# Moving 184 loads of a two-layer diffusion backbone from SyncE's DMA queue to GpSimd's, with the scan's loads fetched one job ahead

## The chip, the cores and the metric

One core of one Trainium2 chip. The metric is the device time of one execution of the whole program in microseconds (us); for this kernel the median of three runs is 2510.61 us, from 2509.51 to 2510.81 us.

## The reference, cut to what matters

Two layers work on 256 context tokens and 256 latent tokens of width 1024. Each layer is a half-step FFN, a mixer and a second half-step FFN; the change lies in the mixer alone.

```python
p = n @ w_in                                   # conv input, q/k/v, z, decay inputs, two gates
y = a * sigmoid(gate)                          # conv branch: depthwise conv of 31 taps along rows of 64
y_conv = silu(layernorm(dwconv(y, 31) + b)) @ conv_proj
# DeltaNet branch: q, k, v by a short conv; chunked scan in both directions, 8 heads of 128
v_new = u - w @ S
o     = (q * exp(g)) @ S + qk @ v_new          # qk = (q k^T) * decay
S     = S * exp(g_last) + (k * exp(g_last - g))^T @ v_new
y_dn  = (rms(o) * silu(z)) @ dn_proj
h    += gate2 * ((sigmoid(gA) * y_conv + sigmoid(gB) * y_dn) @ w_out)
```

Layer 0 produces both streams after the mixer, layer 1 the latent stream alone, so in layer 1 most products have 256 columns where those of layer 0 have 512.

## The kernel before, in words

Everything is kept with channels on the 128 partitions. Every fp32 product is three TensorE products of a high and a low part (`mm3`, L142). A weight tile of 512 KB (`raw`) is loaded by SyncE (L119), split into `whi` by ScalarE (L112) and `wlo` by VectorE (L113). There are three `raw` buffers and three pairs of `whi` and `wlo`, so the weights run at most six tiles ahead of TensorE.

A mixer (`mixer`) runs in these stages:

- The projections of `w_in`. The gated conv input is stored to DRAM (`glu`, L924), and so are `z` and the two gates `ga` and `gb` (from ScalarE's queue, L953). The logs of the decays go through DRAM (`grow`, L496) and come back broadcast over the partitions by eight accumulating DMAs of 512 KB on GpSimd's queue (`R<-grow`, L511); ScalarE takes their exponential in place (L513).
- The depthwise conv (`conv`, L810 to L824). For each of eight channel tiles the input `cx` is read back from `glu` with halos, in layer 0 by five DMAs, in layer 1 by one. VectorE then works through 31 taps (L824). Two `cx` buffers.
- The Gram matrices, and the block-wise inverses of the triangular systems.
- The scan (`scan`). Sixteen jobs, each one chunk of 128 tokens, one direction and four heads; the order alternates over two halves of the heads and two directions. Stages of different jobs are emitted side by side: `prepare` for the job three ahead, `residue` two ahead, `load` and `values` one ahead, `update` for the job itself. `load` reads the masked products `pt` (L739), the broadcast decays `qt` (L743) and the queries `q` (L745), 256 KB each, and VectorE multiplies `qt` by `q` (L746). `pt` and `qt` have two buffers, `q` one. `update` multiplies `qt` with the state `S` (L777) and `pt` with the new values (L778). In layer 1 only the eight jobs of the latent stream have outputs, and so these loads.
- `out_norm`: the outputs are normalised (a power on GpSimd, L883), transposed (L891) and multiplied by `z` (L892), which is loaded again (L888) into three buffers shared by all heads.
- `branch`: products with `conv_proj` and `dn_proj`, multiplied by the gates `g` (L1018). The first branch is stored (`m`, L1023), the second loads it again as `other` (L1009) and adds it (L1020). `g`, `other` and other temporaries share the four buffers `w512`.
- `w_out` and the residual.

A framework orders the instructions of each engine by priority and writes the waits. Each engine's instructions, SyncE's DMA issues included, then run strictly in their order; a DMA that waits for a buffer or for data holds back what stands behind it on its queue. The queues of SyncE, ScalarE and GpSimd move their bytes over the same 16 DMA engines.

Of the kernel before, what the change touches and what calls it, by code (L numbers as in the profile page):

```python
# [46 lines left out]
class Net:  # L47
# [660 lines left out]
    def scan(self, y, S, R, K, qsp, V, o, psp, pool, beside):  # L708


        nc = self.nc
        tile = lambda name, bufs: pool.tile([128, 4, 128], F32, tag=name, name=name, bufs=bufs)
# [15 lines left out]
        def load(g):  # L728
            if not g.last:
                g.kd = tile("kd", 2)  # L730
                pk = self.psx()
                for j in range(4):
                    nc.tensor.transpose(pk[:, j * 128:(j + 1) * 128], K[g.st][:, g.q * 4 + j, g.tok], self.ident)
                for j in range(4):
                    h = g.q * 4 + j
                    nc.scalar.activation(out=g.kd[:, j, :], in_=pk[:, j * 128:(j + 1) * 128], func=AF.Copy, scale=y.kd[:, g.d, g.t, h:h + 1])
            if g.need_o:
                g.pt = tile("pt", 2)
                nc.sync.dma_start(out=g.pt.rearrange("p h i -> p (h i)"), in_=psp[g.t][:, g.d * 1024 + g.q * 512:g.d * 1024 + g.q * 512 + 512])  # L739
                if not g.first:  # L740
                    g.qt, q = tile("qt", 2), tile("q", 1)
                    c0 = g.d * 32 + g.t * 8 + g.q * 4
                    nc.sync.dma_start(out=g.qt.rearrange("p h i -> p (h i)"),  # L743
                                      in_=y.rows[1][c0:c0 + 4, :].rearrange("a b -> (a b)").partition_broadcast(128))
                    nc.sync.dma_start(out=q, in_=qsp[g.st].rearrange("p (h t) -> p h t", h=8)[:, g.hs, g.tok])  # L745
                    nc.vector.tensor_tensor(out=g.qt, in0=g.qt, in1=q, op=ALU.mult)  # L746

        def residue(g):
# [41 lines left out]

        n = len(jobs)
        for i in range(-3, n):
            for off, stage in ((3, prepare), (2, residue), (1, load), (1, values), (0, update)):
                if 0 <= i + off < n:
                    stage(jobs[i + off])
            for f in beside.get(i, ()):
                f()

    def conv(self, y, glu, ysp, ysum, pool, tok):

        nc = self.nc
        ctx = tok.start == 0
        for k in range(KT):
            x = pool.tile([128, 8, 94], F32, tag="cx", name="cx")
            r0 = 0 if ctx else 4
            if ctx:
                c = glu[k][:, 0:256]
                nc.gpsimd.memset(x[:, 0, 0:15], 0.0)
                nc.gpsimd.memset(x[:, 3, 79:94], 0.0)
                nc.sync.dma_start(out=x[:, 0, 15:94], in_=c[:, 0:79])  # L810
                for r in (1, 2):
                    nc.sync.dma_start(out=x[:, r, :], in_=c[:, 64 * r - 15:64 * r + 79])
                nc.sync.dma_start(out=x[:, 3, 0:79], in_=c[:, 177:256])
            nc.gpsimd.memset(x[:, 4:, 0:15], 0.0)
            nc.gpsimd.memset(x[:, 4:, 79:94], 0.0)
            nc.sync.dma_start(out=x[:, 4:, 15:79], in_=glu[k][:, 256:512].rearrange("p (r c) -> p r c", c=64))
            o = pool.tile([128, 512], F32, tag="cy", name="cy")
            dst = o[:, tok].rearrange("p (r c) -> p r c", c=64)
            for j in range(31):
                w, src = y.cdw[:, j, k:k + 1], x[:, r0:, j:j + 64]  # L820
                if j == 0:
                    nc.vector.tensor_scalar(out=dst, in0=src, scalar1=w, scalar2=y.dwb[:, k:k + 1], op0=ALU.mult, op1=ALU.add)
                else:
                    nc.vector.scalar_tensor_tensor(out=dst, in0=src, scalar=w, in1=dst, op0=ALU.mult, op1=ALU.add)  # L824
            nc.sync.dma_start(out=ysp[k][:, tok], in_=o[:, tok])
            if k == 0:
                nc.vector.tensor_copy(out=ysum[:, tok], in_=o[:, tok])
            else:
                nc.vector.tensor_tensor(out=ysum[:, tok], in0=ysum[:, tok], in1=o[:, tok], op=ALU.add)
# [38 lines left out]
    def out_norm(self, y, o, s, zsp, oh, ol):  # L868

        nc = self.nc  # L870
        st, ts = STREAM[s], slice(2 * s, 2 * s + 2)
        so = self.sp.tile([128, 2, 8], F32, tag="so", name="so")
        for q in range(2):
            hs = slice(4 * q, 4 * q + 4)
            for tt in range(2):
                for h in range(4 * q, 4 * q + 4):
                    sq = self.wk.tile([128, 256], F32, tag="sq", name="osq", bufs=2)[:, :128]
                    nc.scalar.activation(out=sq, in_=o[:, 2 * s + tt, h, :], func=AF.Square, accum_out=so[:, tt, h:h + 1])
            sv, rq = so[:, :, hs], y.rq[:, ts, hs]
            nc.vector.tensor_tensor(out=sv, in0=sv, in1=rq, op=ALU.mult)  # L880
            nc.vector.scalar_tensor_tensor(out=sv, in0=sv, scalar=1.0 / 128, in1=rq, op0=ALU.mult, op1=ALU.mult)
            nc.vector.tensor_scalar(out=sv, in0=sv, scalar1=EPS, scalar2=None, op0=ALU.add)
            nc.gpsimd.tensor_tensor(out=sv, in0=sv, in1=self.mhalf[:, :8].rearrange("p (t h) -> p t h", t=2), op=ALU.pow)  # L883
            nc.vector.tensor_tensor(out=sv, in0=sv, in1=rq, op=ALU.mult)
            nc.vector.tensor_tensor(out=o[:, ts, hs, :], in0=o[:, ts, hs, :], in1=sv.unsqueeze(3).to_broadcast([128, 2, 4, 128]), op=ALU.mult)
            for h in range(4 * q, 4 * q + 4):
                z = self.wk.tile([128, 256], F32, tag="t1", name="z", bufs=3)
                nc.sync.dma_start(out=z, in_=zsp[h][:, st])  # L888
                ps = self.psx()
                for tt in range(2):  # L890
                    nc.tensor.transpose(ps[:, tt * 128:(tt + 1) * 128], o[:, 2 * s + tt, h, :], self.ident)  # L891
                nc.vector.scalar_tensor_tensor(out=z, in0=ps[:, :256], scalar=y.onorm, in1=z, op0=ALU.mult, op1=ALU.mult)  # L892
                self.split(oh[:, h, st], ol[:, h, st], z)

    def mixer(self, y, nxt):
        nc, a, l = self.nc, self.a, y.l
        w_in = a["w_in"][l]
        streams = (0, 1) if l == 0 else (1,)
        tok = FULL if l == 0 else STREAM[1]
        dram = lambda name, cols: self.dp.tile([128, cols], F32, name=f"{name}_{l}")  # L900
        hsp = dram("hsp", KT * T)
        psp = [dram(f"psp{t}", 2048) for t in range(4)]
        qsp = [dram(f"q{s}", 2048) for s in range(2)]
        zsp, asp, bsp, glu, ysp, msp = ([dram(f"{nm}{k}", T) for k in range(8)] for nm in ("z", "ga", "gb", "glu", "y", "m"))
        x, xctx = self.n, self.np_ctx
# [11 lines left out]
        for k in range(KT):  # L917
# [3 lines left out]
            t_ = self.w512("glu")  # L921
# [84 lines left out]

        def load(src, name):
            t_ = self.w512(name)
            nc.sync.dma_start(out=t_[:, tok], in_=src[:, tok])  # L1009
            return t_[:, tok]  # L1010

        oh, ol, mh, ml = [None] * 4
# [123 lines left out]
```

## Time and profile before

| | |
|---|---|
| median of three runs | 2510.61 us |
| the profiled execution | 2517.16 us |
| its span, first to last instruction | 2515.4 us |
| TensorE busy | 2410.1 us (96%) |
| VectorE busy | 1774.5 us (71%) |
| ScalarE busy | 956.0 us (38%) |
| GpSimd busy, without its DMA issues | 51.7 us (2%) |
| mean granted TensorE clock | 0.984 |
| moved by SyncE's queue | 371.33 MB |
| moved by GpSimd's queue | 8.39 MB |

The mixer of layer 0 lies between about 420 and 1060 us of the span, that of layer 1 between about 1830 and 2310 us; the FFNs fill the rest. SPq, POOLq and ACTq are the DMA issues of SyncE, GpSimd and ScalarE. "<-" in brackets names what ended the idle time before an instruction. Busy time of TensorE counts modelled ends, so a full slice is not TensorE at its peak.

### The profile page before, as it was taken

How to read it: one execution, taken by the hardware profiler on the slowest of the kernel's cores; microseconds unless marked ns; L12 is line 12 of the kernel's file. 1: busy time of each engine (PE TensorE's matmuls, PEld its weight loads, DVE VectorE, ACT ScalarE, POOL GpSimd, SP SyncE). 2: the span in 40 equal slices, each digit the busy share in tenths (PEclk: the TensorE clock that was granted, in tenths of full speed). 3: DMA queues.
4: the chain of work that ended last, by engine and by line, in shares of the span. 5: the costliest groups of instructions: out<-in, count | busy, mean ns of one | idle time of the engine just before them, and what ended most of it. 6: DMA issues, size and time to landing. Idle time of an engine off the chain costs nothing. (4 is left out here: it accounts for less than half of the span.)

```text
span 2515.4 us, 38318 instructions
## 1 busy us (share of the span) xinstructions
PE 2410.1 (96%) x15099; PEld 2043.3 (81%) x15099; DVE 1774.5 (71%) x3023; ACT 956.0 (38%) x1578; POOL 51.7 (2%) x111
## 2 busy tenths in 40 slices
PE   7999999999999999999999999999988998978998
PEld 5777778787887887887777888778887886878998
DVE  4766777699999665576667564444468999966554
ACT  3222222435443643332222232222245556544443
POOL 0000000100000000000000000000010000000000
PEclk9999999999999999999999999999999999988999
DMA  8556665744644474455555544444466572355664
GB/s 253 165 164 175 173 176 172 170 133 113 207 137 118 145 224 151 116 156 158 163 157 160 152 126 126 126 125 133 120 173 178 169 218 79 108 174 164 198 184 138
DMA packets 566773, 394.61 MB, mean 157 GB/s; under 512 B 27704, under 2 KB 513218, under 8 KB 564930
## 3 DMA queue, kind: packets, MB, share of 16 engines
q1 hardware_dynamic: 555606, 371.33, 51.2%
q0 software_dynamic: 2304, 8.39, 1.7%
q10 hardware_dynamic: 8684, 12.45, 1.5%
q8 instruction: 118, 1.93, 0.3%
q14 instruction: 61, 0.50, 0.1%
HBM read 358.43 MB, written 33.69 MB: 156 GB/s over the span
## 5 line engine op out<-in xcount | busy, mean ns | idle before, releaser
L142 PE MATMUL pm<-nh,whi 128*128 128x512 f32 (+1 forms) x2544 | 907.8, 359 | 23.2 <-ACT whi L112 16.3
L142 PE MATMUL pm<-nh,wlo 128*128 128x512 f32 (+1 forms) x2544 | 903.3, 356 | 2.9 <-DVE wlo L113 2.2
L142 PE MATMUL pm<-nl,whi 128*128 128x512 f32 (+1 forms) x2544 | 903.3, 356 | 0.0
L112 ACT ACTIVATE whi<-raw 128x1024 fp32r<-128x1024 f32 (+1 forms) x450 | 469.1, 1044 | 1109.3 <-PE pm L142 857.7
L113 DVE TENSOR_TENSOR wlo<-raw,whi 128x1024 fp32r<-128x1024 f32 (+1 forms) x450 | 541.1, 1204 | 237.3 <-ACT whi L112 233.2
L142 PEld LDWEIGHTS pm<-nh,whi 128*128 128x128 f32 x2544 | 480.9, 190 | 115.1 <-ACT whi L112 25.1
L142 PEld LDWEIGHTS pm<-nh,wlo 128*128 128x128 f32 x2544 | 480.9, 189 | 79.2 <-DVE wlo L113 4.4
L142 PEld LDWEIGHTS pm<-nl,whi 128*128 128x128 f32 x2544 | 481.3, 190 | 73.6 <-DVE nl L375 1.0
L296 DVE SCALAR_TENSOR_TENSOR aacc<-adaw,sc,aacc 128x512 f32<-128x512 f32 x448 | 312.3, 747 | 164.8 <-DMA adaw<-ada_w_in 164.7
L824 DVE SCALAR_TENSOR_TENSOR cy<-cx,cdw,cy 128x512 f32<-128x512 f32 (+1 forms) x480 | 272.0, 612 | 1.3
L142 PE MATMUL pm<-gh,whi 128*128 128x512 f32 (+1 forms) x770 | 268.8, 349 | 1.7 <-DVE h L380 1.7
L142 PE MATMUL pm<-gl,whi 128*128 128x512 f32 (+1 forms) x770 | 267.4, 347 | 0.0
L142 PE MATMUL pm<-gh,wlo 128*128 128x512 f32 (+1 forms) x770 | 267.3, 347 | 0.0
L142 PEld LDWEIGHTS pm<-gh,whi 128*128 128x128 f32 x770 | 145.7, 189 | 26.4 <-issue 3.4
L142 PEld LDWEIGHTS pm<-gh,wlo 128*128 128x128 f32 x770 | 145.7, 189 | 18.9 <-issue 0.8
L142 PEld LDWEIGHTS pm<-gl,whi 128*128 128x128 f32 x770 | 145.7, 189 | 17.6
L428 DVE TENSOR_TENSOR silu<-silu,pm 128x512 f32<-128x512 f32 (+1 forms) x88 | 54.5, 619 | 77.3 <-PE pm L142 70.2
L380 DVE SCALAR_TENSOR_TENSOR h<-pm,gate,h 128x256 f32<-128x256 f32 x80 | 36.4, 480 | 63.3 <-PE pm L142 63.0
L112 ACT ACTIVATE gh<-silu 128x512 fp32r<-128x512 f32 (+1 forms) x88 | 50.5, 573 | 39.1 <-DVE silu L428 39.0
L374 ACT ACTIVATE nh<-t,mods 128x256 fp32r<-128x256 f32 x88 | 39.9, 502 | 61.1 <-DVE t L371 61.0
L113 DVE TENSOR_TENSOR gl<-silu,gh 128x512 fp32r<-128x512 f32 (+1 forms) x88 | 54.4, 618 | 0.0
L142 PE MATMUL pm<-mh,whi 128*128 128x256 f32 (+1 forms) x152 | 48.3, 320 | 2.2 <-ACT mh L112 2.2
(248 smaller groups left out, 2376.9 us busy)
## 6 DMA issues: line engine op xcount, KB each, us to landing
raw<-ffn_w_in SPq DMA_DIRECT2D x208, 512.0 KB, 4.1
adaw<-ada_w_in SPq DMA_DIRECT2D x144, 512.0 KB, 4.0
raw<-w_in_in SPq DMA_DIRECT2D x130, 512.0 KB, 4.2
raw<-ffn_w_in SPq DMA_DIRECT2D x64, 448.0 KB, 4.3
R<-grow POOLq DMA_DIRECT2D x16, 512.0 KB, 13.9
raw<-conv_proj_in SPq DMA_DIRECT2D x16, 512.0 KB, 6.5
raw<-dn_proj_in SPq DMA_DIRECT2D x16, 512.0 KB
raw<-w_out_in SPq DMA_DIRECT2D x16, 512.0 KB, 4.1
```

The lines of the kernel that those rows point to most:

```text
L112: nc.scalar.activation(out=hi, in_=x, func=AF.Copy)
L113: nc.vector.tensor_tensor(out=lo, in0=x, in1=hi.bitcast(F32), op=ALU.subtract)
L142: nc.tensor.matmul(ps, lhsT=u[:, j, :], rhs=v[:, k, tok], start=k == 0 and p == 0, stop=k == n - 1 and p == 2)
L296: nc.vector.scalar_tensor_tensor(out=st.acc[:, s], in0=wt[:, j], scalar=c, in1=st.acc[:, s], op0=ALU.mult, op1=ALU.add)
L374: nc.scalar.activation(out=nh[:, k, st], in_=t1, func=AF.Identity, bias=B)
L380: self.nc.vector.scalar_tensor_tensor(out=self.h[:, m, st], in0=ps[:, st], scalar=y.gate[:, q, m, s:s + 1], in1=self.h[:, m, st], op0=ALU. ...
L428: nc.vector.tensor_tensor(out=t, in0=t, in1=pb[:, tok], op=ALU.mult)
L824: nc.vector.scalar_tensor_tensor(out=dst, in0=src, scalar=w, in1=dst, op0=ALU.mult, op1=ALU.add)
```

## The change

184 loads go from SyncE's queue to GpSimd's: 48 of `cx` (40 in layer 0), 24 of `pt`, 20 of `qt`, 20 of `q`, 24 of `z`, 32 of `g` and 16 of `other`. Weights, and all stores, stay where they were. In the scan, the loads become a stage of their own, `fetch`, which is emitted ahead of `residue`, for the job one ahead, and `q` gets a second buffer.

```diff
@@ scan
                     nc.scalar.activation(out=g.kd[:, j, :], in_=pk[:, j * 128:(j + 1) * 128], func=AF.Copy, scale=y.kd[:, g.d, g.t, h:h + 1])
+
+        def fetch(g):
             if g.need_o:
                 g.pt = tile("pt", 2)
-                nc.sync.dma_start(out=g.pt..., in_=psp[g.t][...])
+                nc.gpsimd.dma_start(out=g.pt..., in_=psp[g.t][...])
                 if not g.first:
-                    g.qt, q = tile("qt", 2), tile("q", 1)
+                    g.qt, q = tile("qt", 2), tile("q", 2)
-                    nc.sync.dma_start(out=g.qt..., in_=y.rows[1][...].partition_broadcast(128))
+                    nc.gpsimd.dma_start(out=g.qt..., in_=y.rows[1][...].partition_broadcast(128))
-                    nc.sync.dma_start(out=q, in_=qsp[g.st]...)
+                    nc.gpsimd.dma_start(out=q, in_=qsp[g.st]...)
                     nc.vector.tensor_tensor(out=g.qt, in0=g.qt, in1=q, op=ALU.mult)
-            for off, stage in ((3, prepare), (2, residue), (1, load), (1, values), (0, update)):
+            for off, stage in ((3, prepare), (1, fetch), (2, residue), (1, load), (1, values), (0, update)):
@@ conv: the four halo loads of the context and the one of the latent rows
-                nc.sync.dma_start(out=x[...], in_=glu[k][...])
+                nc.gpsimd.dma_start(out=x[...], in_=glu[k][...])
@@ out_norm
-                nc.sync.dma_start(out=z, in_=zsp[h][:, st])
+                nc.gpsimd.dma_start(out=z, in_=zsp[h][:, st])
@@ mixer, load of g and other
-            nc.sync.dma_start(out=t_[:, tok], in_=src[:, tok])
+            nc.gpsimd.dma_start(out=t_[:, tok], in_=src[:, tok])
```

The order on TensorE, VectorE and ScalarE hardly moves; SyncE and GpSimd are where it does. Line numbers of the changed kernel are two higher from the scan's loads on.

SyncE before the change, in the scan of layer 1. The eight jobs of the latent stream are called 1 to 8; `q_18953` is the q of job 4, `qt_18995`, `pt_18993` and `q_18996` belong to job 5, `qt_19038`, `pt_19036` and `q_19039` to job 6, and `y7`, `yc` to the conv branch:

```order
L745 DMA q_18953<-q1_1_14804 128x4x128
L743 DMA qt_18995<-grow11_15149 128x512
L739 DMA pt_18993<-psp2_1_14801 128x512
L745 DMA q_18996<-q1_1_14804 128x4x128
L825 DMA y7_1_14844<-cy_18486 128x256
L743 DMA qt_19038<-grow11_15149 128x512
L739 DMA pt_19036<-psp2_1_14801 128x512
L845 DMA yc_19118<-y0_1_14837 128x256
L845 DMA yc_19122<-y1_1_14838 128x256
L845 DMA yc_19128<-y2_1_14839 128x256
L745 DMA q_19039<-q1_1_14804 128x4x128
```

The q of a job is the last of its loads, behind the qt and pt of the same job and, for job 6, behind three loads of the conv branch.

GpSimd in the changed kernel, the same place: `qt_18880` and `pt_18878` are of job 3, `pt_18931` and `qt_18933` of job 4, `q_18987`, `qt_18986` and `pt_18984` of job 5, `q_19030`, `qt_19029` and `pt_19027` of job 6, `q_19062` of job 7:

```order
L745 DMA qt_18880<-grow11_15149 128x512
L741 DMA pt_18878<-psp2_1_14801 128x512
L747 DMA q_18987<-q1_1_14804 128x4x128
L741 DMA pt_18931<-psp3_1_14802 128x512
L745 DMA qt_18933<-grow11_15149 128x512
L745 DMA qt_18986<-grow11_15149 128x512
L741 DMA pt_18984<-psp2_1_14801 128x512
L747 DMA q_19030<-q1_1_14804 128x4x128
L745 DMA qt_19029<-grow11_15149 128x512
L741 DMA pt_19027<-psp2_1_14801 128x512
L747 DMA q_19062<-q1_1_14804 128x4x128
```

The q of a job now stands ahead of the qt and pt of its own job, for job 5 also ahead of those of job 4, and no load or store of the conv branch stands between.

GpSimd in the changed kernel, where the decays of layer 0 are read back (`R`); before the change only the power of L342 stood ahead of the `R` rows:

```order
L342 TENSOR_TENSOR rs_3297<-ms_3295,mhalf_91 128x2
L812 DMA cx_6797<-glu0_0_3367 128x79
L814 DMA cx_6797<-glu0_0_3367 128x94 x2
L815 DMA cx_6797<-glu0_0_3367 128x79
L818 DMA cx_6797<-glu0_0_3367 128x4x64
L812 DMA cx_6841<-glu1_0_3368 128x79
L814 DMA cx_6841<-glu1_0_3368 128x94 x2
L815 DMA cx_6841<-glu1_0_3368 128x79
L818 DMA cx_6841<-glu1_0_3368 128x4x64
L511 DMA R0_3394<-grow00_3681 128x1024 x4
L511 DMA R1_3395<-grow00_3681 128x1024 x4
```

Ten loads of the conv's first two channel tiles now stand ahead of the eight `R` loads; in layer 1 it is two.

## Rows read from the trace of the kernel before

**Rows 1.** The page, part 1: busy time, share of the span, instructions.

```profile
PE 2410.1 (96%) x15099; PEld 2043.3 (81%) x15099; DVE 1774.5 (71%) x3023; ACT 956.0 (38%) x1578; POOL 51.7 (2%) x111
```

**Rows 2.** Busy time by stretch: PE, PEld, DVE, ACT, POOL, granted clock, DMA share, GB/s.

```profile
940.00:980.00 40.00, 35.34 (x163) 27.93 (x164) 21.71 (x43) 13.03 (x46) 3.27 (x2) 0.90 0.51 160
1880.00:1900.00 20.00, 8.65 (x40) 7.95 (x41) 6.61 (x11) 8.90 (x11) 1.56 (x2) 0.67 0.98 220
2190.00:2216.00 26.00, 18.59 (x123) 17.44 (x122) 17.24 (x48) 8.18 (x29) 0.00 (x0) 0.84 0.75 234
2254.00:2278.00 24.00, 23.52 (x200) 23.32 (x200) 15.11 (x25) 9.12 (x12) 0.00 (x0) 1.00 0.86 250
```

**Rows 3.** Waits of ScalarE in time order, decays of layer 1 (start, us, instruction).

```profile
1872.17 1.06 ACT L513 ACTIVATE R<-R 128x1024 f32<-128x1024 f32 x1 [4.47 <-DMA R<-grow]
...
1894.66 1.06 ACT L112 ACTIVATE whi<-raw 128x1024 fp32r<-128x1024 f32 x1 [7.54 <-DMA raw<-w_in_in]
```

**Rows 4.** Waits of TensorE, 2186 to 2222 us (us in total, times, longest).

```profile
PE px L777 <- issue: 4.5, 2, 4.0
PE px L777 <- DVE qt L746: 2.7, 2, 2.3
```

**Rows 5.** VectorE in order of time, scan of layer 1.

```profile
2199.98 0.69 DVE L746 TENSOR_TENSOR qt<-qt,q 128x512 f32<-128x512 f32 x1 [2.75 <-DMA q<-q]
...
2211.38 0.69 DVE L746 TENSOR_TENSOR qt<-qt,q 128x512 f32<-128x512 f32 x1 [2.32 <-DMA q<-q]
```

**Rows 6.** SyncE's queue in order of time, scan of layer 1.

```profile
2194.81 0.37 SPq L745 DMA_DIRECT2D q<-q  x1
...
2206.51 0.37 SPq L745 DMA_DIRECT2D q<-q  x1
```

**Rows 7.** TensorE in order of time: first L777 of jobs 4, 5, 8.

```profile
2190.65 0.46 PE L777 MATMUL px<-S,qt 128*128 128x128 f32 x2 [0.55 <-issue]
...
2194.61 0.49 PE L777 MATMUL px<-S,qt 128*128 128x128 f32 x2
...
2212.17 0.77 PE L777 MATMUL px<-S,qt 128*128 128x128 f32 x2 [4.00 <-issue]
```

**Rows 8.** Waits of TensorE, 930 to 980 us.

```profile
PE px L891 <- DVE z L892: 4.5, 5, 1.5
PE px L777 <- DVE qt L746: 2.9, 1, 2.9
```

**Rows 9.** DMA issues of the whole span: count, KB each, median us to landing.

```profile
qt<-grow SPq DMA_DIRECT2D x20, 256.0 KB, 4.0
q<-q SPq DMA_DIRECT2D x20, 256.0 KB, 3.0
...
z<-z SPq DMA_DIRECT2D x24, 128.0 KB, 3.8
...
other<-m SPq DMA_DIRECT2D x8, 128.0 KB, 3.4
```

**Rows 10.** Tile R, 1855 to 1912 us: GpSimd's issues (ns min/median/max), landings (us).

```profile
L511 POOL DMA_DIRECT2D R<-grow x8: 862/898/1567, 1866.0 to 1884.1; - x8
...
DMA to landing us min/median/max: 6.2/12.0/17.0
```

**Rows 11.** Tile R, 440 to 510 us: GpSimd's issues in layer 0.

```profile
L511 POOL DMA_DIRECT2D R<-grow x8: 1578/2244/3400, 465.3 to 469.8; - x8
```

**Rows 12.** SyncE's queue, 440 to 505 us: loads of the conv's second tile.

```profile
462.06 0.54 SPq L810 DMA_DIRECT2D cx<-glu  x1
```

**Rows 13.** SyncE's queue, 2140 to 2320 us: first and last of eight loads of other.

```profile
2257.78 0.42 SPq L1009 DMA_DIRECT2D other<-m  x1
...
2282.78 0.58 SPq L1009 DMA_DIRECT2D other<-m  x1
```

More of the change, by code (lines that the diff above doesn't have):

```diff
@@ L736, in load @@
                     nc.scalar.activation(out=g.kd[:, j, :], in_=pk[:, j * 128:(j + 1) * 128], func=AF.Copy, scale=y.kd[:, g.d, g.t, h:h + 1])
+        def fetch(g):
             if g.need_o:
                 g.pt = tile("pt", 2)
-                nc.sync.dma_start(out=g.pt.rearrange("p h i -> p (h i)"), in_=psp[g.t][:, g.d * 1024 + g.q * 512:g.d * 1024 + g.q * 512 + 512])
+                nc.gpsimd.dma_start(out=g.pt.rearrange("p h i -> p (h i)"), in_=psp[g.t][:, g.d * 1024 + g.q * 512:g.d * 1024 + g.q * 512 + 512])
                 if not g.first:
-                    g.qt, q = tile("qt", 2), tile("q", 1)
+                    g.qt, q = tile("qt", 2), tile("q", 2)
                     c0 = g.d * 32 + g.t * 8 + g.q * 4
-                    nc.sync.dma_start(out=g.qt.rearrange("p h i -> p (h i)"),
+                    nc.gpsimd.dma_start(out=g.qt.rearrange("p h i -> p (h i)"),
                                       in_=y.rows[1][c0:c0 + 4, :].rearrange("a b -> (a b)").partition_broadcast(128))
-                    nc.sync.dma_start(out=q, in_=qsp[g.st].rearrange("p (h t) -> p h t", h=8)[:, g.hs, g.tok])
+                    nc.gpsimd.dma_start(out=q, in_=qsp[g.st].rearrange("p (h t) -> p h t", h=8)[:, g.hs, g.tok])
                     nc.vector.tensor_tensor(out=g.qt, in0=g.qt, in1=q, op=ALU.mult)
@@ L809, in conv @@
                 nc.gpsimd.memset(x[:, 3, 79:94], 0.0)
-                nc.sync.dma_start(out=x[:, 0, 15:94], in_=c[:, 0:79])
+                nc.gpsimd.dma_start(out=x[:, 0, 15:94], in_=c[:, 0:79])
                 for r in (1, 2):
-                    nc.sync.dma_start(out=x[:, r, :], in_=c[:, 64 * r - 15:64 * r + 79])
-                nc.sync.dma_start(out=x[:, 3, 0:79], in_=c[:, 177:256])
+                    nc.gpsimd.dma_start(out=x[:, r, :], in_=c[:, 64 * r - 15:64 * r + 79])
+                nc.gpsimd.dma_start(out=x[:, 3, 0:79], in_=c[:, 177:256])
             nc.gpsimd.memset(x[:, 4:, 0:15], 0.0)
             nc.gpsimd.memset(x[:, 4:, 79:94], 0.0)
-            nc.sync.dma_start(out=x[:, 4:, 15:79], in_=glu[k][:, 256:512].rearrange("p (r c) -> p r c", c=64))
+            nc.gpsimd.dma_start(out=x[:, 4:, 15:79], in_=glu[k][:, 256:512].rearrange("p (r c) -> p r c", c=64))
             o = pool.tile([128, 512], F32, tag="cy", name="cy")
```

## Prediction

> **What bounds the kernel now.** I begin with busy time. TensorE counts 96% of the span [rows 1], so a load that lands earlier is worth something only where TensorE stands still for it. The table by stretch shows where that is in the mixers [rows 2]: two stretches of the scans and what follows them (940 to 980 us in layer 0, 2190 to 2216 us in layer 1, with TensorE busy for 35.3 of 40 and 18.6 of 26 us), and the stretch in which the decays of layer 1 are read back (8.7 of 20 us).
>
> The views of waits then say who is late. In the decay stretch ScalarE, whose instructions run in order, waits 4.47 us for an `R` load and later 7.54 us for a weight [rows 3], while the 16 DMA engines are 0.98 busy: bytes are short there, not issue slots, and the change moves no byte away. In layer 1's scan, TensorE waits 4.5 and 2.7 us ahead of L777 [rows 4]. VectorE in order of time names the cause: the product of `qt` and `q` (L746) waits for `q`, twice [rows 5]. It can't come earlier: `q` has one buffer, so its load is issued only when the product before has ended, 2206.51 us for the product that starts at 2211.38 us [rows 5, 6]. SyncE's order in the section on the change shows the same: a q comes last, and behind what the conv branch wants. In layer 0 the like wait is 2.9 us, and the transposes wait another 4.5 us for `z` [rows 8].
>
> **The sum, against the profiled execution's 2517.16 us**, which is 6.55 us above the median of 2510.61 us.
>
> *Scan of layer 1.* With two buffers q is asked for a job earlier, and nothing of the conv branch stands before it. Undisturbed, job 5 follows job 4 by 2194.61 - 2190.65 = 3.96 us [rows 7]. At that pace job 8 starts 3 x 3.96 = 11.9 us after job 5, at 2206.5 us, and not at 2212.17 us: 5.7 us. Can `qt` follow? Its load waits for L777 two jobs before, then lands in 4.0 us from SyncE [rows 9]; the product takes 0.69 us [rows 5] and the 16 products L777 and L778 about 1.8 us, 123 matmuls being 13.8 us at 0.112 us each. That is 6.5 us for two jobs, under 7.9 us: it can. The granted clock there is 0.84 [rows 2], so 32% of 26 us, 8.3 us, ran at 1.2 GHz and cost 4.2 us. The low clock comes after these stalls, but idle time behind the scan stays; I take half, 2.1 us. Together **-7.8 us**. Bounds: no clock and a landing of 6.2 us as the quickest `R` load [rows 10], which is twice the bytes and adds on the way: 6.2 + 0.69 + 1.8 = 8.7 us for two jobs, job 8 at 2207.7 us, -4.5 us; the whole clock, -9.9 us.
>
> *Scan of layer 0.* The 2.9 us at L777 [rows 8] go, as the loads no longer queue behind stores of `m` that wait for VectorE: **-2.9 us** (bounds 0 and -6.9 us, with the 4.0 us that 40 us at a clock of 0.90 cost). The other loads of this scan lie beside products of `conv_proj`: nothing.
>
> *The decays.* GpSimd gets ten `cx` loads ahead of the `R` loads in layer 0. Those of the first tile are long gone; the five of the second can go once its `glu` has landed, which was so at 462.06 us [rows 12]. GpSimd's issues followed each other by (469.8 - 465.3) / 7 = 0.64 us, and one alone took 0.862 us [rows 10, 11]. Five take 3.2 to 4.3 us and end at 465.3 to 466.4 us; the first `R` load went at 465.3 us. In layer 1 it is one load. No cover here: ScalarE stands still for `R`. **+0.5 us** for both. Upper bound: the `cx` loads with four runs a partition could cost as four, 3.4 us each, so +3.7 and +3.4 us; lower bound 0.
>
> *z, g and other.* Three buffers for `z`, four for `g` and `other`: each load waits for the use of an older one, so landing time is on the path when TensorE has nothing else. The loads of `other` in layer 1 come (2282.78 - 2257.78) / 7 = 3.57 us apart [rows 13], where 24 products of a branch need 24 / 200 x 24 = 2.9 us [rows 2]: loads set the pace. I take the landing as unchanged, for the nearest rows are the same loads from SyncE, 3.4 and 3.8 us [rows 9], and price it at **0**. Bounds: at q's 3.0 us and at `R`'s 6.2 us. `other` makes 4 rounds (eight branches, two in flight), `z` 2 rounds in layer 1 (five loads behind the first three) and 4.3 in layer 0, of which I count half, as products of other branches run beside them: 4 x 2.8 + 4.2 x 2.4 = +21.3 us above, 4 x 0.4 + 4.2 x 0.8 = -5.0 us below.
>
> *Weights and conv input.* Six tiles of weights are ready or on their way, so SyncE's waits for loads were covered already; `cx` has two buffers and 31 taps of time. If that cover goes, in the decay stretch, the missing thing is bytes. Nothing.
>
> Sum: -7.8 - 2.9 + 0.5 = **-10.2 us**: 2507.0 us profiled, **2500.4 us** median.
>
> The quickest landing from GpSimd's queue in these rows is 6.2 us, for an accumulating load [rows 10]; no row has a plain one. The Trainium skill (DMA: Bandwidth & Descriptors, section Specifications) speaks against the change: first byte about 1 us on GpSimd's path and about 0.6 us on SyncE's. By that, an estimate, 0.4 us in each of the 8.2 rounds costs 3.3 us, and the sum would be -6.9 us, 2503.7 us; that plain loads are so slow no run here shows yet.
>
> **The rivals.**
>
> *Slower: landing.* If a plain load from GpSimd lands in 6.2 us, `z` and `other` pay 21.3 us, the scans give 4.5 + 2.9 us and the decays take 0.5 us: +14.4 us, **2525.0 us**. It decides from 10.2 / 8.2 = 1.2 us a landing on. For it: the only loads of that queue landed in 6.2 to 17.0 us [rows 10]. Against: they were 512 KB each, added to their target, in a stretch with the DMA engines 0.98 busy [rows 2].
>
> *No change: issue.* A `q` load has four runs a partition; if each costs what one run costs now, 4 x 0.862 = 3.4 us, GpSimd needs 3.4 + 0.86 + 0.86 = 5.1 us a job, more than 3.96 us. Job 8 starts at 2210.0 us: -2.2 us and no clock; layer 0 -2.9 us; decays up to +7.1 us: +2.0 us, **2512.6 us**.
>
> *Half the gain: the move does nothing.* The DMA engines are the same, so if what held layer 0's loads was bytes (0.51 of them busy there [rows 2] speaks against it), only q's second buffer counts: -7.8 + 0.5 = -7.3 us, **2503.3 us**. The Trainium skill (DMA: Bandwidth & Descriptors, section Issuing engines are not separate DMA queues) says that issuing from several engines saves only the sequencer's time to issue.
>
> *More.* The clock returns wholly in both scans (another 2.1 and 4.0 us) and `z` and `other`, no longer behind 512 KB of weights, land as q does (5.0 us): -21.3 us, **2489.3 us**.
>
> **How the numbers follow.** Forecast 0.38; slower by landing 0.24; no change by issue 0.18; the move does nothing 0.10; more 0.10. About 0.2%, 5.0 us, can be told from no change: under 2505.6 us is faster, above 2515.6 us slower. Faster: 0.36 of the forecast, 0.10 and 0.10 of the two further gains and a little of the issue case, 0.57. Slower: most of the landing case and some of the issue case, 0.23. The rest, 0.20, is the same. The range from 2490 to 2516 us takes in the forecast, the issue case and the gains, and leaves out most of the landing case. The likeliest case alone, with its bounds for the scans and the decays, spans 2495 to 2506 us.
>
> **What would show it.** Right: L746 no longer waits for `q`, job 8's L777 follows job 5's by about 12 us, the clock of that stretch is above 0.84, TensorE's 2.9 us at L777 in layer 0 are gone, and the first `R` load goes within 1 us of before, measured from the store of `grow`. Wrong: `z` or `other` from GpSimd landing above 5 us with transposes or products waiting for them; POOL issues of `q` above 2 us; ScalarE waiting longer for `R`.

## The result, and the profile after

The changed kernel takes 2530.97 us (median of four runs, 2526.17 to 2532.52), the kernel before beside it 2510.45 us: a ratio of 1.0079, 95% interval 1.0062 to 1.0097. It is slower by 0.8%, where 2500.4 us was forecast and a range up to 2516 us. The profiled execution took 2526.17 us (span 2524.5 us) and is the quickest of the four; what the others spend more is in no trace of that measurement, but the same kernel was profiled again below.

Page, part 1 of the changed kernel (busy time, share, instructions), answering to [rows 1]:

```profile
PE 2410.6 (95%) x15099; PEld 2043.7 (81%) x15099; DVE 1775.2 (70%) x3023; ACT 956.0 (38%) x1578; POOL 158.3 (6%) x295
```

TensorE does the same work in the same time; the loss is idle time. GpSimd's busy time contains its DMA issues here: 184 more for 106.6 us, 0.58 us each.

The issues that moved (page, part 6: KB each, median us to landing), answering to [rows 9]:

```profile
qt<-grow POOLq DMA_DIRECT2D x20, 256.0 KB, 4.6
q<-q POOLq DMA_DIRECT2D x20, 256.0 KB, 4.6
...
z<-z POOLq DMA_DIRECT2D x24, 128.0 KB, 2.7
...
other<-m POOLq DMA_DIRECT2D x8, 128.0 KB, 4.1
```

A plain load from GpSimd's queue lands in much the same time as one from SyncE's: `z` in 2.7 us instead of 3.8, `qt` in 4.6 instead of 4.0, `other` in 4.1 instead of 3.4, `q` in 4.6 instead of 3.0. So the loss isn't one price on every load.

The table by stretch, in the columns of [rows 2] (PE, PEld, DVE, ACT, POOL, granted clock, DMA share, GB/s):

```profile
940.00:980.00 40.00, 33.26 (x173) 27.31 (x172) 19.69 (x42) 12.25 (x45) 10.30 (x15) 0.93 0.45 144
1880.00:1900.00 20.00, 10.35 (x65) 9.85 (x65) 8.21 (x13) 9.06 (x11) 1.69 (x2) 0.74 1.09 243
2190.00:2216.00 26.00, 17.72 (x125) 15.82 (x123) 17.37 (x49) 7.02 (x26) 4.76 (x9) 0.87 0.70 228
2254.00:2278.00 24.00, 21.53 (x170) 21.48 (x171) 13.23 (x23) 7.88 (x11) 6.67 (x13) 0.93 0.72 217
```

The stretch of the decays looks no worse here, both scans, which were to gain, look worse (33.26 against 35.34 us of TensorE, 17.72 against 18.59), and so does the first branch of layer 1, for which nothing was forecast. But stretches fixed in time cut other work out of each trace: in the second profile of the changed kernel, below, TensorE is busy for 22.03 us from 2190 to 2216 us. So the losses are better read from the same matmuls in both traces.

**Where the time went.** Matmuls of the same line and names, as often in one trace as in the other, can be paired: the n-th with the n-th. The table gives how much the median difference of their start times to the trace of before grows over four stretches (bounds in the time of before). Kernels that change nothing in a stretch show from -3.0 to +1.8 us there; that is the scatter of one profile against another. It can be more: scan_only and scan_hlate have the same instructions in the same order up to layer 1's scan, and differ by 3.9 us in the second column. All kernels but the first are the experiments.

| kernel | conv of layer 0, 530 to 830 us | scan of layer 0 and transposes, 910 to 1020 | scan of layer 1 to its transposes, 2172 to 2227 | first branch of layer 1, 2227 to 2268 | ratio, 95% interval |
|---|---|---|---|---|---|
| changed kernel | +5.8 | +3.4 | +4.2 | +4.8 | 1.0079 (1.0062 to 1.0097) |
| after_again, the same | +5.6 | +3.6 | +5.4 | +6.6 | 1.0087 (1.0072 to 1.0102) |
| after_hlate | +5.1 | +1.9 | +0.6 | +6.7 | 1.0062 (1.0050 to 1.0074) |
| h_pool | +3.5 | +7.5 | -0.3 | +6.0 | 1.0076 (1.0064 to 1.0089) |
| no_g | +5.5 | +2.2 | +5.4 | +6.4 | 1.0076 (1.0063 to 1.0089) |
| no_z | +3.3 | +3.7 | +5.5 | +2.4 | 1.0061 (1.0042 to 1.0080) |
| repaired | -0.5 | +1.8 | +0.3 | +6.5 | 1.0051 (1.0037 to 1.0066) |
| scan_only | -1.0 | -1.1 | +5.2 | -0.9 | 1.0026 (1.0016 to 1.0036) |
| scan_hlate | -0.2 | +2.8 | +1.8 | -0.7 | 1.0014 (1.0006 to 1.0023) |
| rest_only | +4.8 | -2.9 | +0.5 | +6.0 | 1.0030 (1.0018 to 1.0042) |
| cx_only | +5.8 | -1.2 | -1.3 | -0.4 | 1.0022 (1.0012 to 1.0032) |
| cx_3buf | +2.6 | +0.9 | -3.0 | -0.4 | 1.0015 (1.0005 to 1.0025) |
| g_only | +0.2 | -1.2 | -0.9 | +4.0 | 1.0018 (1.0007 to 1.0028) |
| z_only | +1.8 | +2.5 | -0.7 | +5.8 | 1.0033 (1.0022 to 1.0044) |
| sp_all | +0.2 | -3.8 | -1.6 | +1.1 | 0.9990 (0.9979 to 1.0002) |
| sp_q2 | +0.1 | -3.3 | -1.8 | -0.5 | 0.9995 (0.9982 to 1.0007) |

Four losses, one in each stretch, make 18.2 us in the first profile of the changed kernel and 21.2 us in the second; the medians differ by 20.5 and 22.0 us. The first profile's whole span is only 9.1 us longer because its other stretches were together some 9 us shorter than in the profile of before. A profile is one execution, and the four columns of a row come within -2.0 to +5.6 us of the difference of its medians (repaired: 8.1 us in the columns, 13.7 us between the medians); what is missing is in no one of the four stretches. The bound between the last two columns lies among transposes whose place in the order changes, and moves some us from one to the other: at 2240 us instead of 2227 it is about +3.1 and +5.9 for the changed kernel, +2.2 and +3.6 for h_pool, where the table has -0.3 and +6.0.

**The scan of layer 1.** Views of the changed kernel in order of time, with one row of the trace of before (start, us, instruction, idle time before it and what ended it). SyncE's queue behind the conv branch's loads:

```profile
2198.72 0.38 SPq L1037 DMA_DIRECT2D h<-hsp  x1
```

The same load before:

```profile
2207.28 0.32 SPq L1035 DMA_DIRECT2D h<-hsp  x1
```

GpSimd's queue at that moment:

```profile
2198.49 0.54 POOL L745 DMA_DIRECT2D qt<-grow  x1 [2.04 <-PE px L780]
2199.02 0.54 POOL L741 DMA_DIRECT2D pt<-psp  x1
2199.55 0.76 POOL L747 DMA_DIRECT2D q<-q  x1
2202.06 0.54 POOL L745 DMA_DIRECT2D qt<-grow  x1 [1.76 <-PE px L780]
```

VectorE, the product for the first of these two `qt`:

```profile
2207.24 0.69 DVE L748 TENSOR_TENSOR qt<-qt,q 128x512 f32<-128x512 f32 x1 [6.93 <-DMA qt<-grow]
```

TensorE behind it:

```profile
2208.25 2.08 PE L765 MATMUL pm<-bv,R 128*128 128x128 f32 x8 [5.82 <-DVE bv L759]
```

`h<-hsp` is the 2 MB load of the residual stream, which is wanted only after `w_out`. Before, it stood on SyncE's queue behind the scan's last `q` and went at 2207.28 us. With the scan's loads gone from that queue it goes 8.6 us earlier, 0.23 us after the seventh job's `qt`. That `qt` lands 8.6 us after its issue, VectorE waits 6.93 us for it, and since VectorE runs in order, what TensorE needs from it (`bv`) waits too. The first theory was that this early load makes the `qt` late.

**The scan of layer 0.** GpSimd's queue, 937 to 946 us:

```profile
937.05 0.76 POOL L747 DMA_DIRECT2D q<-q  x1 [5.69 <-DVE qt L748]
937.80 0.54 POOL L745 DMA_DIRECT2D qt<-grow  x1
938.33 0.54 POOL L741 DMA_DIRECT2D pt<-psp  x1
944.54 0.54 POOL L1011 DMA_DIRECT2D g<-ga  x1 [5.67 <-DMA m<-g]
945.07 0.54 POOL L745 DMA_DIRECT2D qt<-grow  x1
945.60 0.54 POOL L741 DMA_DIRECT2D pt<-psp  x1
```

A `g` load waits 5.67 us until the store of `m` from its buffer has landed, and the next `qt` and `pt` stand behind it. Before, SyncE's queue stood still there too, from 933.46 to 936.95 us, ahead of a `g` load with a `pt` and a `qt` behind it. So moving the loads along moved this wait along.

It is not the wait that the prediction priced. The 2.9 us of [rows 8] end with this product; the first row is the issue of its `qt` on SyncE's queue, both of the trace of before:

```profile
932.97 0.49 SPq L743 DMA_DIRECT2D qt<-grow  x1
...
939.20 0.69 DVE L746 TENSOR_TENSOR qt<-qt,q 128x512 f32<-128x512 f32 x1 [4.02 <-DMA qt<-grow]
```

From its issue to the product are 6.2 us, where the median landing is 4.0 us [rows 9]: by that, an estimate, some 2.2 of the 2.9 us are a slow landing, and not a place in the queue.

### The profile page after: what moved, and what is told of

It reads as the page before. It is cut to its first block, busy times and chain, and to the rows that moved or that the text cites. A ratio compares the mean times of both kernels' runs of the same rounds, so it can differ in the third digit from the quotient of the medians.

```text
span 2524.5 us, 38358 instructions
## 1 busy us (share of the span) xinstructions
PE 2410.6 (95%) x15099; PEld 2043.7 (81%) x15099; DVE 1775.2 (70%) x3023; ACT 956.0 (38%) x1578; POOL 158.3 (6%) x295
## 5 line engine op out<-in xcount | busy, mean ns | idle before, releaser
L342 POOL TENSOR_TENSOR rs<-ms,mhalf 128x2 f32<-128x2 f32 (+1 forms) x13 | 11.0, 846 | 1453.2 <-DVE ms L340 1453.2
```

Source lines behind the costliest of these rows:

```text
L342: nc.gpsimd.tensor_tensor(out=rs[:, :nt], in0=ms[:, :nt], in1=self.mhalf[:, :nt], op=ALU.pow)
```

## The experiments

Theories A to M are told in the expectations; each kernel is the changed kernel, or the one before, with the edit shown. Those that start from the kernel before have the scan's loads in the stage `fetch` too, emitted right behind `load`, where they stood. Line numbers are those of the changed kernel. Ratios stand in the table above.

### Half of the change at a time

**scan_only**: `cx`, `z`, `g` and `other` stay on SyncE's queue.

```diff
-  nc.gpsimd.dma_start(out=x[...], in_=glu...)
+  nc.sync.dma_start(out=x[...], in_=glu...)
-  nc.gpsimd.dma_start(out=z, in_=zsp[h][:, st])
+  nc.sync.dma_start(out=z, in_=zsp[h][:, st])
-  nc.gpsimd.dma_start(out=t_[:, tok], in_=src[:, tok])
+  nc.sync.dma_start(out=t_[:, tok], in_=src[:, tok])
```

> Only pt, qt and q on GpSimd's queue, with the new stage and q's second buffer; cx, z, g and other stay on SyncE's. Theory A: the h load is early here too, so the end of layer 1's scan has the same late qt, and the time is 2 to 8 us above before, 2512 to 2518 us; z, g and other cost nothing more. Theory B: every scan load is late, the same sign, but qt lands late (over 6 us) in all jobs and not in the last two alone. Theory D (the loss comes from z, g, other and cx): 2502 to 2508 us.

**rest_only**: the scan as before.

```diff
-  g.qt, q = tile("qt", 2), tile("q", 2)
+  g.qt, q = tile("qt", 2), tile("q", 1)
-  nc.gpsimd.dma_start(out=g.pt...)      # and qt, q
+  nc.sync.dma_start(out=g.pt...)
-  ((3, prepare), (1, fetch), (2, residue), (1, load), (1, values), (0, update))
+  ((3, prepare), (2, residue), (1, load), (1, fetch), (1, values), (0, update))
```

> Only cx, z, g and other on GpSimd's queue; the scan as before (loads on SyncE's, q with one buffer). Theory A: the h load stays behind the scan's q, so the scan keeps its time and what remains is the conv input and the gates: 2510 to 2518 us. Theory D (the loss is that of z, g, other and cx): 2525 to 2532 us.

**sp_all**: the new stage and q's second buffer, no load moved (both edits, `gpsimd` back to `sync` everywhere).

> Only the new stage order and q's second buffer; all loads stay on SyncE's queue. Theory A and B both: the q wait of layer 1's scan is gone and the h load stays behind the scan's loads, so the time is 4 to 8 us under before: 2502 to 2506 us. Theory C (q's wait was not worth anything, since what follows the scan is late anyhow): 2509 to 2512 us.

scan_only lost 0.26% and rest_only 0.30%, so neither half alone is the loss, and theory D, which put all of it on the second half, falls. Of the four stretches, only the end of layer 1's scan loses in scan_only (+5.2 us). sp_all gained 0.10%, an interval that reaches to no change, so theory C's band is the one it fits; its profile has 1.6 us less in layer 1's scan, not 7.8, and 3.8 us less in layer 0's, hardly more than the scatter.

### Is it the early load of h?

**h_pool**: the changed kernel with h's load on GpSimd's queue too.

```diff
-  nc.sync.dma_start(out=self.h.rearrange("p k t -> p (k t)"), in_=hsp)
+  nc.gpsimd.dma_start(out=self.h.rearrange("p k t -> p (k t)"), in_=hsp)
```

> The changed kernel, with one load more on GpSimd's queue: the 2 MB load of h (L1037), which there stands behind the scan's last loads. Theory A (early h): in the changed kernel SyncE's queue no longer waits inside the scan, so the h load goes at 2198.7 us instead of 2207.3 us and takes the bytes of the last two jobs' qt and pt (landing 9.9 and 11.5 us). Then qt lands in under 6 us in layer 1, the 6.2 us gap of TensorE at 2202 us goes, and the time is 6 to 10 us under the changed kernel's 2531.0 us: 2521 to 2525 us. Theory B (GpSimd's queue lands late by itself): qt of the last jobs still lands in 8 to 10 us, the time stays at 2529 to 2533 us.

The time did not fall. But the edit didn't do what its expectation says: on GpSimd's queue the load stood ahead of the last job's `pt` and `qt`. GpSimd's queue in h_pool:

```profile
2212.55 0.76 POOL L747 DMA_DIRECT2D q<-q  x1
2213.30 0.53 POOL L1037 DMA_DIRECT2D h<-hsp  x1
2215.29 0.54 POOL L741 DMA_DIRECT2D pt<-psp  x1 [1.46 <-PE px L780]
2215.82 0.54 POOL L745 DMA_DIRECT2D qt<-grow  x1
```

TensorE's waits there (us in total, times, longest):

```profile
PE px L779 <- DVE qt L748: 7.7, 1, 7.7
```

Now it is the eighth job's `qt` that is late, for 7.7 us. In layer 0 h's load also went ahead of others, and that stretch lost 7.5 us. The run does not test theory A as it was meant to; where the late `qt` moved speaks for A.

**after_hlate** and **scan_hlate**: in layer 1 a copy that h's load overwrites, and so has to wait for, holds that load until the last output of the scan is there. The second one has it on top of scan_only.

```diff
+  if l == 1:
+      nc.vector.tensor_copy(out=self.h[:, 0, 0:16].rearrange("p (a b) -> p a b", b=8), in_=o[:, 2:4, :, 0])
   nc.sync.dma_start(out=self.h.rearrange("p k t -> p (k t)"), in_=hsp)
```

> The changed kernel, but in layer 1 a copy of 16 numbers a partition from o to the buffer of h goes ahead of h's load, so that load waits for the scan's last output; TensorE's order up to the last FFN is that of the changed kernel. Theory A (early h): qt of the last two jobs lands in under 6 us (9.9 us in the changed kernel), the gap of 6.2 us at 2202 us goes, and the time is 3 to 7 us under the changed kernel's, a ratio to before of 1.005 to 1.007 where that had 1.0079. Theory B (GpSimd's queue lands late by itself): qt still lands in 8 to 10 us, ratio 1.007 to 1.009.

> pt, qt and q alone on GpSimd's queue, with the new stage and q's second buffer, and h held back in layer 1 as in the run beside it. Without h held back this had a ratio of 1.0026. Theory A: without the late qt at the end of layer 1's scan 4 to 6 us less, ratio 1.000 to 1.001, and TensorE's waits at L765 and L779 in that scan are under 3 us each. Theory B: no difference, 1.002 to 1.004.

SyncE's queue of after_hlate:

```profile
2218.43 0.32 SPq L1039 DMA_DIRECT2D h<-hsp  x1
```

Landings of tile `qt` in layer 1, after_hlate:

```profile
DMA to landing us min/median/max: 3.8/4.5/7.5
```

The same row of the changed kernel:

```profile
DMA to landing us min/median/max: 4.0/5.5/9.9
```

With h held back, the stretch falls from +4.2 and +5.4 to +0.6 us, and from +5.2 to +1.8 us on top of scan_only; the ratios fall from 1.0079 and 1.0087 to 1.0062, and from 1.0026 to 1.0014, between the bands of A and B (the intervals overlap, the stretches are further apart than the scatter). TensorE's wait for `bv` at L765 falls from 6.0 to 2.9 us, and from 7.2 to 1.8 us. The pace of the jobs shows it best: from the first L779 of job 5 to that of job 8 it took 17.56 us before and 17.39 us in the changed kernel, but 13.89 us in after_hlate and 14.0 us in sp_all. Theory A holds for 3.4 to 4.8 us of this stretch: the last two `qt` landed in 5.5 and 4.5 us, where they took 8.6 and 9.9 us in the changed kernel. The 7.5 us in the row of after_hlate are those of the scan's second `qt`, at 2147.7 us, which landed in 7.0 us in the changed kernel.

### The second half by itself

**cx_only**, **g_only** and **z_only**: before, with one kind of load moved.

```diff
-  nc.sync.dma_start(out=x[...], in_=glu...)            # cx_only: L812 to L818
+  nc.gpsimd.dma_start(out=x[...], in_=glu...)
-  nc.sync.dma_start(out=t_[:, tok], in_=src[:, tok])   # g_only: L1011
+  nc.gpsimd.dma_start(out=t_[:, tok], in_=src[:, tok])
-  nc.sync.dma_start(out=z, in_=zsp[h][:, st])          # z_only: L890
+  nc.gpsimd.dma_start(out=z, in_=zsp[h][:, st])
```

> Only the 48 cx loads on GpSimd's queue; the rest as before. Theory E (cx lands later behind GpSimd's own instructions, and VectorE, 97 to 100% busy beside the conv of layer 0, has no time to give): VectorE waits 3 to 4 us more for cx at L824, TensorE loses 2 us between 560 and 660 us and 2 us at 760 us, ratio 1.0010 to 1.0025. Theory F (cx has two buffers and 31 taps of time, as the prediction had it): ratio 0.9995 to 1.0005.

> Only g and other on GpSimd's queue (48 loads); the rest as before. Theory D (a g load that waits for its buffer holds back nothing here, but is itself issued late): what is lost is the 6 us after 2240 us that the run with cx, z, g and other on GpSimd's queue lost, ratio 1.0015 to 1.003. Theory G (that loss came from z on GpSimd's queue, or from the order of the conv branch's norm): ratio 0.9995 to 1.0010.

> Only the 24 loads of z on GpSimd's queue; the rest as before. Theory J (order): with z on GpSimd's queue the framework puts VectorE's and ScalarE's work beside layer 1's first branch in another order (the third and later splits of a weight ahead of the conv branch's, the products with the gates last), and this makes the 6 us that every kernel with z there lost between 2220 and 2260 us: TensorE stands still about 4 us for L1020 after 2245 us, ratio 1.0015 to 1.003. Theory K (z is not it; the loss there came from the new scan order and from g): ratio 0.9990 to 1.0005, no such gap.

Each of them is slower by itself. Their losses are 0.22, 0.18 and 0.33%, more than rest_only's 0.30% together: those of `g` and of `z` lie at the same place and do not add up.

By the bands of the expectations theory E fits cx_only, D g_only and J z_only, whose ratio is just above J's band; F, G and K fall.

*cx.* VectorE's waits (us in total, times, longest) in the conv of layer 0, the changed kernel's; before, this was 1.2 us:

```profile
DVE cy L824 <- DMA cx<-glu: 4.1, 3, 1.6
```

VectorE is 97 to 98% busy from 530 to 760 us in the changed kernel, so it has little time to make up for a tap that starts late. TensorE waits at two places more than before: near 565 us for ScalarE (1.1 us, in cx_only 2.6 us, before 0.3 us; but 1.6 us also in z_only, scan_hlate and sp_q2, with `cx` on SyncE's queue), and at L665, where the profile gives no releaser:

```profile
PE px L665 <- issue: 4.8, 1, 4.8
```

That wait is 2.2 us before, 4.0 us in cx_only and 2.1 to 2.6 us in the other kernels with `cx` on SyncE's queue.

**cx_3buf**: cx_only and a third buffer.

```diff
-  x = pool.tile([128, 8, 94], F32, tag="cx", name="cx")
+  x = pool.tile([128, 8, 94], F32, tag="cx", name="cx", bufs=3)
```

> Only the 48 cx loads on GpSimd's queue, and a third buffer for cx. Theory E (VectorE waits for cx since the load starts only when the second buffer is free and lands 1 to 2 us too late): the waits of VectorE at L824 for cx fall from 3.5 us to under 1 us in the conv of layer 0, TensorE's losses there go, ratio 0.999 to 1.001 where two buffers had 1.0022. Theory I (the conv's place in VectorE's order, or GpSimd's issues themselves, make the loss): ratio 1.0015 to 1.003 with no wait for cx.

VectorE's waits for `cx` are gone, the loss of the conv falls from 5.8 to 2.6 us, but L665 still waits 4.0 us and the ratio of 1.0015 is not told apart from 1.0022. In repaired (below), with the same third buffer, L665 waits 2.0 us and the stretch loses nothing. By the bands that is theory I. cx_3buf and repaired have one and the same order of VectorE's instructions in this stretch, so +2.6 and -0.5 us are two measures of one thing, below the 3.3 to 5.8 us of every kernel with two buffers and `cx` on GpSimd's queue. That moving `cx` costs is shown; how is not. A rival of VectorE's waits was not tried: with `cx` moved, some 90 of the 570 VectorE instructions between 440 and 830 us stand at another place in the order, and with the third buffer the order is another again. What L665 waits for stays open too.

*z and g.* z_only and before start the branch of layer 1 at nearly the same time, and VectorE then does the same work in another order. VectorE before:

```profile
2236.93 3.49 DVE L113 TENSOR_TENSOR wlo<-raw,whi 128x1024 fp32r<-128x1024 f32 x3
2240.34 0.42 DVE L113 TENSOR_TENSOR yl<-yn,yh 128x256 fp32r<-128x256 f32 x1
2240.67 0.41 DVE L1018 SCALAR_TENSOR_TENSOR g<-g,pm 128x256 f32<-128x256 f32 x1
2241.00 0.42 DVE L113 TENSOR_TENSOR yl<-yn,yh 128x256 fp32r<-128x256 f32 x1
...
2250.95 0.83 DVE L1018 SCALAR_TENSOR_TENSOR g<-g,pm 128x256 f32<-128x256 f32 x2 [0.21 <-DMA g<-gb]
```

VectorE in z_only:

```profile
2236.89 3.50 DVE L113 TENSOR_TENSOR wlo<-raw,whi 128x1024 fp32r<-128x1024 f32 x3 [0.17 <-ACT whi L112]
2240.30 0.42 DVE L113 TENSOR_TENSOR yl<-yn,yh 128x256 fp32r<-128x256 f32 x1
2240.64 1.27 DVE L863 SCALAR_TENSOR_TENSOR yn<-yc,v,yr 128x256 f32<-128x256 f32 x3
2243.25 1.22 DVE L113 TENSOR_TENSOR wlo<-raw,whi 128x1024 fp32r<-128x1024 f32 x1 [1.34 <-ACT whi L112]
2244.39 0.42 DVE L113 TENSOR_TENSOR yl<-yn,yh 128x256 fp32r<-128x256 f32 x1
2245.28 0.42 DVE L1020 SCALAR_TENSOR_TENSOR g<-g,pm 128x256 f32<-128x256 f32 x1 [0.47 <-DMA g<-gb]
...
2252.93 1.07 DVE L1020 SCALAR_TENSOR_TENSOR g<-g,pm 128x256 f32<-128x256 f32 x3
```

The fourth `yl`, of eight, stands behind another weight (2244.39 against 2240.34 us) and the second gate's product with it (2245.28 against 2240.67 us). These steps give back buffers of `w512` and PSUM, so later gates are asked for later, and TensorE waits. Its waits in this stretch before:

```profile
PE pm L142 <- DVE g L1018: 1.7, 1, 1.7
```

And in z_only:

```profile
PE pm L142 <- DVE g L1020: 5.2, 2, 3.0
```

`z` itself lands in 2.5 us there. This order stands in z_only, rest_only, the changed kernel, after_hlate, no_g and repaired, and in none with `z` on SyncE's queue; these six lose 4.8 to 6.7 us there, the kernels with both `z` and `g` on SyncE's queue between -0.9 and +1.1. It isn't the only way: g_only has nearly the order of before and loses 4.0 us, as L1020 is late (TensorE waits 3.6 us); and h_pool, with `z` and `g` moved, has nearly that order too and loses 6.0 us (3.6 us with the later bound). That the order alone makes z_only's loss was not tried by itself.

**no_g** and **no_z**: the changed kernel with `g` and `other`, or `z`, back on SyncE's queue.

```diff
-  nc.gpsimd.dma_start(out=t_[:, tok], in_=src[:, tok])   # no_g
+  nc.sync.dma_start(out=t_[:, tok], in_=src[:, tok])
-  nc.gpsimd.dma_start(out=z, in_=zsp[h][:, st])          # no_z
+  nc.sync.dma_start(out=z, in_=zsp[h][:, st])
```

> The changed kernel with g and other back on SyncE's queue (48 loads); cx, z and the scan's loads stay on GpSimd's. Theory H (in layer 0 a g load that waits until the store of m has landed stands on GpSimd's queue ahead of pt and qt of the scan, so the queue waits where SyncE's had waited before): TensorE's waits for qt at L779 between 930 and 960 us are under 1.5 us in all, and with the 0.0018 that g and other alone cost the ratio falls by 0.0025 to 0.004 against the changed kernel's. Theory A alone: it falls by 0.001 to 0.002, with the waits at L779 still there.

> The changed kernel with z back on SyncE's queue. Theory J: the order beside layer 1's first branch is that of before again, no gap of 4 us after 2245 us, and the ratio falls by 0.002 to 0.003 under the changed kernel's (1.0079 and 1.0087 on two chips), to 1.005 to 1.0065. Theory K: 1.007 to 1.009.

**after_again** is the changed kernel once more, beside no_g.

> The changed kernel itself, unaltered, on the same chip as the runs beside it, to have one measure for all. Theory A with its parts: ratio to before 1.006 to 1.009 again, qt of layer 1's last jobs landing in 8 us or more, TensorE waiting 2 to 8 us for qt at L779 between 935 and 960 us. If the loss of the first measurement was the chip's, 1.000 to 1.004.

after_again confirms the first measurement. no_z: the old order is back, the branch loses 2.4 us and not 4.8 to 6.6, the ratio is in theory J's band; its interval overlaps the changed kernel's. no_g: TensorE's waits for `qt` at L779 between 930 and 980 us are gone (3.7 us in after_again), as theory H says, but one of 2.2 us for `pt` has come, and one of 4.0 us for `z` stays; the stretch goes from +3.6 to +2.2 us, within the scatter, and the ratio falls by 0.0011 and not by 0.0025 or more. So a `g` load that waits does hold back `qt`, but no price of it can be told from nothing: scan_only and scan_hlate, both with `g` on SyncE's queue, wait 0.7 and 3.4 us for `qt` there, and lose -1.1 and +2.8 us. What makes layer 0's scan slower stays open.

**repaired**: no_g, the held h and the third `cx` buffer together.

> The changed kernel with the three costs taken away together: g and other on SyncE's queue, h held back in layer 1, a third buffer for cx. If they are the loss, the ratio is 0.999 to 1.002; if each only makes way for another wait, 1.003 to 1.006.

It gives back 0.36 of 0.87%, so it falls into the band of "each only makes way for another wait". Two of the four losses are gone in its row of the table (conv -0.5, scan of layer 1 +0.3 us), that of the branch, with `z` on GpSimd's queue, is still there (+6.5 us).

### Why the second buffer gains so little

**sp_q2**: before, with q's second buffer and nothing else.

```diff
-  g.qt, q = tile("qt", 2), tile("q", 1)
+  g.qt, q = tile("qt", 2), tile("q", 2)
```

> One thing alone: q's second buffer, with the old stage order and all loads on SyncE's queue. Theory L (what the second buffer gains in layer 1's scan is lost right behind it, as VectorE's work for the conv branch's norm, which before ran while VectorE waited for q, then stands between the scan's last product and the transposes): the waits of L748 for q go, the gap before the first transposes grows from 5.4 to 6 us or more, ratio 0.998 to 1.000. Theory M (the stage order is what spoils it): ratio 0.9965 to 0.998.

VectorE no longer waits for `q`, job 8 follows job 5 in 13.14 us instead of 17.56. And yet the time is that of before. TensorE's longest wait behind the scan in sp_q2:

```profile
PE px L893 <- DVE so L882: 7.3, 1, 7.3
```

VectorE in that wait:

```profile
2204.73 0.68 DVE L784 TENSOR_TENSOR o<-px,o 128x512 f32<-128x512 f32 x1
2205.33 0.41 DVE L854 TENSOR_TENSOR ysum<-ysum,ysq 128x256 f32<-128x256 f32 x1
2205.67 1.09 DVE L848 TENSOR_TENSOR yc<-yc,mean 128x256 f32<-128x256 f32 x3
2206.67 0.16 DVE L882 TENSOR_TENSOR so<-so,r 128x8 f32<-128x8 f32 x1
2206.84 0.42 DVE L854 TENSOR_TENSOR ysum<-ysum,ysq 128x256 f32<-128x256 f32 x1
...
2210.08 1.23 DVE L887 TENSOR_TENSOR o<-o,so 128x1024 f32<-128x1024 f32 x1
```

Before, VectorE did the conv branch's norm (L848, L854) while it waited for `q`. Now that work stands between the scan's last output and the chain of `out_norm` that the transposes wait for: TensorE's gap there, from start to start of two matmuls, is 7.60 us where it was 5.39, and the next one 2.50 us where it was 1.20. Of the 4.4 us won in the scan 3.5 us are lost right behind it. Theory L holds; the stage order is not what spoils it.

No kernel here beats the one before by more than its interval. sp_all, at 0.9990, comes nearest.

## Why the prediction was wrong

- **Scan of layer 1, -7.8 us: wrong by sign.** The step that failed is "nothing of the conv branch stands before it": I asked what the moved loads stand behind on their new queue, and not what had stood behind them on the old one. The answer is in the queue's order, a row below the last `q`: 2 MB of `h`. With it the stretch loses 4.2 to 5.5 us; held back, +0.3 to +1.8 us. The pace of 3.96 us a job (11.9 us for three) was somewhat too quick: 13.1 to 14.9 us in the runs with q's second buffer whose h load goes behind all loads of the scan. One figure behind it stands in no row: the 16 products L777 and L778 were put at 1.8 us, 0.112 us each, where [rows 2] have 18.59 us for those 123 matmuls, 0.151 us each, and the trace of before has 2.0 us for a job's 16 at 2.4 GHz and 3.7 us at 1.2 GHz. With 2.0 us the check comes out the same, with 3.7 us (8.4 us for two jobs) it doesn't.
- **The scan's end was taken for the path's end.** The sum had "idle time behind the scan stays" in it, and that idle time grew: VectorE's waits for `q` had not been empty. In sp_q2 that turned some 4 us into about 1. The clock's 2.1 us did not come either: from 2190 to 2216 us the granted clock was 0.87 after 0.84, but from 2190 to 2240 us, with what follows the scan, 0.80 and 0.79 in the two profiles of the changed kernel after 0.83.
- **Scan of layer 0, -2.9 us: wrong.** The step that failed is "the loads no longer queue behind stores of `m` that wait for VectorE". It took the 2.9 us for a place in a queue, and by the estimate above 2.2 us of them were a slow landing; with `g` and `other` off SyncE's queue (g_only) TensorE still waits 3.8 us there. It also overlooked that `g`'s loads wait for the landing of those same stores and moved along: 5.67 us on GpSimd's queue. The stretch lost 3.4 and 3.6 us, of which no run shows the cause.
- **Decays, +0.5 us: right.** GpSimd's eight `R` loads in layer 0 went 3.6 us earlier than before by the clock of their trace (461.7 and 465.3 us; TensorE was 3.7 us ahead there), and the stretch of layer 1 shows no loss.
- **z, g, other, 0: the landing was right, the price was not.** They landed in 2.7 to 4.1 us (medians), and yet the branch lost 5 to 7 us. The step that failed was to price landings alone, and to take the order on TensorE, VectorE and ScalarE as unmoved because it "hardly moves" over the whole program: some 170 of VectorE's 3023 instructions moved, 41 of them between 2140 and 2330 us. That this order makes the loss is the likeliest account, not a shown one.
- **cx, nothing: wrong**, +3.3 to +5.8 us with two buffers. The cover named, two buffers and 31 taps, was gone three times for up to 1.6 us, on an engine that is 97 to 98% busy there. Whether these waits or VectorE's other order make the loss is open.
- **The rivals.** The slower one had the sign and, at 2525.0 us, missed by 6 us only. That is luck, as its mechanism, a landing of 6.2 us for plain loads, is refuted. The issue rival is refuted as well: a `q` load occupies GpSimd for 0.76 us, not 3.4. "Only the second buffer counts" was far off for the changed kernel, but the nearest to what the buffer alone did: 7.3 us were expected, 1 to 3 us measured.

The Trainium skill (DMA: Bandwidth & Descriptors, section Specifications) was quoted for a first byte after about 1 us on GpSimd's path and about 0.6 us on SyncE's. The rows neither bear the difference out nor refute it: `z` landed 1.1 us sooner, `q` 1.6 us later, and more than 0.4 us hangs on what else moves at that moment. Its section Issuing engines are not separate DMA queues, that all issuers' transfers interleave on the same 16 engines, is what the `h` row shows: 2 MB from SyncE's queue took `qt`, on GpSimd's, from the 4.0 us of [rows 9] to 9.9 us.

## What to carry to other kernels

Before loads leave a queue, read what stands behind them there: a large transfer that nobody waits for may have been held back by them, and will go at once and take the bytes of those that are waited for. Where a framework orders the instructions, compare its order at the places where TensorE already waits, not over the whole program. And before a wait is priced as a gain, look at what the waiting engine would do next, and whether other work had been done in that wait.

## What was not expected of the hardware

- Plain loads of 128 KB from GpSimd's queue landed in 2.7 to 4.1 us and those of 256 KB in 3.3 to 4.6 us (medians), against 6.2 to 17.0 us for the accumulating loads of 512 KB on the same queue, in a stretch with the DMA engines 0.98 busy [rows 2, 10].
- Issuing costs GpSimd 0.54 us for a load of one run a partition and 0.76 us for four, in the rows shown; the `q` issues of SyncE's queue took 0.37 us [rows 6].
- TensorE stood still for 2 to 5 us in L665, among products of 32x32, with no releaser that the profile shows; which kernels stand long there goes mostly with `cx` on GpSimd's queue, and no run says why.
